# Loading x of tiles 0 and 1 and the first weights through one DMA queue in order of use, with chunks in four parts and seven idle matmuls

## The chip, the cores and the metric

The kernel runs on the 8 cores of one Trainium2 chip; every core has one of the eight sequences of the batch. The time of a run is the device time in microseconds (us) of the slowest core. Executions fall in two states, whatever the kernel: in the slow one the cores of one die, or of both, show a lower granted TensorE clock and the run is some per cent longer, up to 3317 us. Only fast runs are compared.

Each run also lists the span of each core, from its first to its last instruction. I use two figures beside the time: the span of the slowest core, which makes the time, and the mean span of the eight cores, which is less at the mercy of one core.

## The reference

One residual block of a streaming encoder, on x of 8 sequences x 4096 frames x 1024 channels. Only its first part bears on the change:

```python
def reference(x, norm_ffn1, ffn1_w_gate, ffn1_w_up, ffn1_w_down, ...):
    # macaron first half-step FFN
    x = x + 0.5 * swiglu(rmsnorm(x, norm_ffn1[l]), ffn1_w_gate[l], ffn1_w_up[l], ffn1_w_down[l])
    # ... gated attention and gMLP mixers, second half-step FFN ...
    return rmsnorm(x, norm_final)

def swiglu(h, w_gate, w_up, w_down):
    return (jax.nn.silu(h @ w_gate) * (h @ w_up)) @ w_down
```

## The kernel before

A core works on tiles of 512 frames; x of a tile lies in SBUF as 128 partitions x 8 rows x 512 columns of f32 (2.10 MB). A gate-and-up weight chunk ("fsrc") is 128 x 4096, written as bf16 (1.05 MB) into the ring of weight buffers RING. Its eight slices of 512 columns go with the eight rows of x: 32 matmuls for one chunk and one tile. Tiles 0 and 1 start together: chunk 0 for tile 0, chunk 1 for tile 0, then the same two chunks for tile 1.

The weights are issued by GpSimd (the software DMA queue), x by SyncE (a hardware queue). `p.dma` and `p.add` record an operation with what it reads and writes, and a helper derives the semaphore waits from that. So `reads=[("X", 0, 4)]` on a weight load is a pure wait: GpSimd may not issue chunk 1 before row 4 of x of tile 0 has landed.

```python
# pump(): weight chunk k into its ring slot
if k < 2:
    for j in range(4):                       # chunks 0 and 1 in four parts
        part = (slice(None), slice(j * 1024, (j + 1) * 1024))
        p.dma("pool", lambda e, o=dst[part], i_=src[part]: e.dma_start(out=o, in_=i_),
              reads=[("X", 0, 4)] if k else (), writes=res[2 * j:2 * j + 2], sem=f"first{k}{j}")
else:                                        # later chunks in one piece
    p.dma("pool", lambda e, dst=dst, src=src: e.dma_start(out=dst, in_=src),
          reads=[("X", 1, 3)] if k == 2 else (), writes=res, sem=f"slotq{i}")
# ... cut ...
# gu_chunk(), tile 0 with chunk 0
for kc in range(8):
    nraw(t, 0, kc)                           # VectorE: XT = X * gain, f32 to bf16
    for j in range(4):
        mm(j, kc)                            # TensorE
    if kc:
        nsq(t, kc - 1, "dve")                # ScalarE squares, VectorE adds into ACC
nsq(t, 7, "dve")
nstat(RS[t], ("RS", t))                      # TensorE sums ACCR over partitions; ScalarE makes YA
# ... while chunk 1 goes on: scalings and additions for tile 1, one row at a time
nraw(1, 0, d)                                # VectorE
nsq(1, d)                                    # ScalarE squares, GpSimd adds
# ... cut ...
# the start of the program
load_x(0, False)                             # SyncE, eight rows
pump(2)                                      # chunks 0 and 1
load_x(1, False, lambda d: c1[5])            # SyncE waits for the third part of chunk 1
pump()                                       # chunks 2, 3 and 4
```

So the kernel before sets the order x of tile 0 with chunk 0, chunk 1, x of tile 1, chunk 2 by three waits: GpSimd for x of tile 0, SyncE for chunk 1, GpSimd for x of tile 1.

Of the kernel before, what the change touches and what calls it, by code (L numbers as in the profile page):

```python
# [17 lines left out]
T = 512  # L18
NT = S_LEN // T
NGR = 46  # L20
NSEM = 12
EPS = 1e-6
R_MAX = 1e18
BIAS_MAX = 10.0
# [6 lines left out]
def _keep_at():  # L31

    at = {("ffs", 0, f2): int(n < 4) for n, f2 in enumerate(F2J)}
    at |= {("wds", 0, d): 1 for d in range(8)}
    at |= {("wis", g): n for g, n in zip((4, 3, 2, 0, 1), (1, 0, 1, 0, 1))}
    at |= {("mgs", d): n for d, n in enumerate((0, 1, 1, 2, 0, 1, 2, 1))}
    at |= {("wos", 0): 1, ("wos", 1): 2}
    at |= {("ffs", 1, f2): n for f2, n in zip(F2, (1, 2, 0, 2, 1, 2, 1, 0, 2, 1, 2))}
    at |= {("wds", 1, d): n for d, n in enumerate((1, 2, 2, 1, 0, 2, 1, 2))}
    return at  # L40


KEEP_AT = _keep_at()


class _Op:
# [156 lines left out]
def build_nc(n_tiles=NT):  # L203
# [28 lines left out]
    with ExitStack() as st:  # L232
# [5 lines left out]
        def bank(i):  # L238
            return PS[i // 2][:, (i % 2) * 512:(i % 2 + 1) * 512]
# [56 lines left out]
        def run(p, dry):  # L296
# [4 lines left out]
            place = {}  # L301
# [22 lines left out]
            def pump(stop=1 << 30):  # L324
                while nxt[0] < min(stop, len(chunk_order)) and (general[0] or nxt[0] < fast_len[0]):
# [17 lines left out]
                    if chunk not in converted:  # L343
                        u = uses.get(chunk, 0)
                        uses[chunk] = u + 1
                        if k < 2:
                            for j in range(4):
                                part = (slice(None), slice(j * 1024, (j + 1) * 1024))
                                p.dma("pool", lambda e, o=dst[part], i_=src[part]: e.dma_start(out=o, in_=i_),
                                      reads=[("X", 0, 4)] if k else (), writes=res[2 * j:2 * j + 2], sem=f"first{k}{j}")  # L350
                        else:
                            p.dma("pool", lambda e, dst=dst, src=src: e.dma_start(out=dst, in_=src),
                                  reads=[("X", 1, 3)] if k == 2 else (), writes=res, sem=f"slotq{i}")
                        if u >= KEEP_AT[chunk]:
                            converted.add(chunk)
                            pending_wb[k] = (chunk, scr, dst, i)
                    else:
                        p.dma("sp", lambda e, dst=dst, scr=scr: e.dma_start(out=dst, in_=scr),
                              reads=[("SCR", chunk)], writes=res, sem=f"slot{i}")
# [24 lines left out]
                    del live[k]  # L384
                    pump()

            def load_x(t, paced=True, after=None):
                b = t % 3
                step = 4 if paced else 1
                for d in range(0, 8, step):  # L390
                    p.dma("sp", lambda e, d=d: e.dma_start(out=X[b][:, d:d + step, :],
                                                        in_=x_d[:, d:d + step, t * T:(t + 1) * T]),
                          reads=[after(d)] if after else [], writes=[("X", b, i) for i in range(d, d + step)],
                          sem=f"x{b}{d}", paced=paced)

            dn = [0]

# [648 lines left out]
                    pass  # L1046

            p.dma("act", lambda e: e.dma_start(out=G4[:], in_=g4_d), writes=["G4"], sem="c0")
            load_x(0, False)
            if not dry:  # L1050
                pump(2)
                c1 = place[1][1]
                load_x(1, False, lambda d: c1[5])
                pump()
            p.add("dve", lambda e: e.memset(ONESR[:].bitcast(F32), 1.0), writes=["ONESR"])
            p.add("dve", lambda e: e.memset(EPSB[:], EPS), writes=["EPSB"])
            p.add("dve", lambda e: e.memset(NHALF[:], -0.5), writes=["NHALF"])
# [178 lines left out]
```

## Time and profile before

| | before |
|---|---|
| first three timed runs | 2795.04, 2960.86, 3316.71 us (one fast, two slow) |
| fast runs, all later calls (27) | 2787.2 to 2796.3 us, median 2790.8 |
| TensorE busy in the profiled run | 97% of 2786.6 us |
| first real matmul, mean of 8 cores | 9.9 us |
| first statistics matmul (tile 0) | 22.4 us |
| second statistics matmul (tile 1), from which TensorE is full | 46.3 us |

The page counts busy time by engine, divides the span into 40 slices, and follows back the chain that ended last; the prediction shows those lines. The lines of GpSimd (POOL) are its time-ordered view on core 5: start, duration, engine and line, what, how many; in brackets the idle time before and what ended it.

```profile
1.56 2.32 POOL L349 DMA_DIRECT2D RING<-fsrc  x4 [0.87 <-POOLq L204]
16.13 2.21 POOL L349 DMA_DIRECT2D RING<-fsrc  x4 [12.25 <-DMA X<-xT]
29.49 1.58 POOL L352 DMA_DIRECT2D RING<-fsrc  x3 [11.15 <-DMA X<-xT]
31.07 1.29 POOL L477 TENSOR_TENSOR ACC<-ACC,TG 128x512 f32<-128x512 f32 x1
```

Two of the three ordering waits are here (12.25 and 11.15 us for X).

### The profile page before, as it was taken

What the parts mean: (1) busy time and instruction counts of PE and PEld (TensorE: products, weight loads), DVE (VectorE), ACT (ScalarE), POOL (GpSimd) and SP (SyncE); (2) the same over time, 40 slices, a digit from 0 to 9 for tenths busy, and PEclk for the clock granted to TensorE, in tenths of its full rate; (3) what the DMA queues carried; (4) which work ended last, traced back from release to release, by engine and by line L of the source; (5) the groups of instructions that cost most, each with busy time, mean ns of one, the idle gap of its engine ahead of it and who ended that gap; (6) DMA issues with size and microseconds to landing.
All of it is one profiled execution on the core that took longest, in us unless ns stands there. A gap on an engine that the chain in (4) does not pass through costs nothing.

```text
span 2786.6 us, 38337 instructions; the slowest of 8 cores (2777.5 to 2786.6 us)
## 1 busy us (share of the span) xinstructions
PE 2702.4 (97%) x13034; PEld 1209.5 (43%) x13034; DVE 1183.2 (42%) x1940; ACT 910.7 (33%) x1466; POOL 311.5 (11%) x356
## 2 busy tenths in 40 slices
PE   7998999999999999999999999999999999999997
PEld 2443444434444444444444444444444444444343
DVE  5643543435334453344533445424443244455332
ACT  3323432225322353223432244322442225314321
POOL 2001120101111011110011001010011101100111
PEclk9999999999999999999999999999999999999998
DMA  9868989977797556974344634446344453443352
GB/s 190 188 124 178 212 179 178 201 241 149 185 202 222 166 144 175 231 231 148 133 151 144 212 129 136 152 149 210 122 142 150 159 169 130 144 148 123 119 186 79
DMA packets 87124, 461.91 MB, mean 166 GB/s; under 512 B 9224, under 2 KB 9224, under 8 KB 55056
## 3 DMA queue, kind: packets, MB, share of 16 engines
q1 hardware_dynamic: 70656, 365.68, 38.6%
q0 software_dynamic: 16128, 93.69, 21.1%
q8 instruction: 112, 1.84, 0.3%
q14 instruction: 84, 0.69, 0.1%
q10 hardware_dynamic: 144, 0.02, 0.0%
HBM read 488.03 MB, written 65.01 MB: 198 GB/s over the span
## 4 chain that ended last, share of the span: by engine, by line
PE 88%; DMA 5%; DVE 3%; ACT 2%; issue 2%; DVEq 0%; SPq 0%; POOL 0%; ACTq 0%; POOLq 0%
PE ps L547 40%; PE ps L618 19%; PE ps L930 8%; PE ps L671 6%; PE ps L684 4%; PE ps L940 4%; PE ps L959 4%; PE ps L835 2%; DMA ffs<-RING 2%; PE ps L812 1%; ACT E L818 1%; DMA RING<-fsrc 1%; DMA RING<-wd 1%; DMA RING<-ffs 1%; DMA X<-xT 1%
## 5 line engine op out<-in xcount | busy, mean ns | idle before, releaser
L547 PE MATMUL ps<-XT,RING 128*128 128x512 bf16 x5632 | 1232.5, 380 | 25.4 <-DMA RING<-fsrc 10.6
L547 PEld LDWEIGHTS ps<-XT,RING 128*128 128x128 bf16 x5632 | 547.6, 98 | 691.8 <-issue 41.3
L618 PE MATMUL ps<-HT,RING 128*128 128x512 bf16 x2656 | 607.6, 380 | 9.2 <-DVE HT L571 7.1
L477 POOL TENSOR_TENSOR ACC<-ACC,TG 128x512 f32<-128x512 f32 x174 | 224.2, 1289 | 1710.0 <-ACT TG L474 1709.6
L571 DVE TENSOR_TENSOR HT<-ps,TG 128x512 bf16<-128x512 f32 x332 | 229.2, 690 | 386.6 <-PE ps L547 338.9
L618 PEld LDWEIGHTS ps<-HT,RING 128*128 128x128 bf16 x2656 | 252.9, 98 | 317.4 <-issue 36.3
L474 ACT ACTIVATE TG<-X 128x512 f32<-128x512 f32 x224 | 140.1, 627 | 404.0 <-DVE X L624 329.5
L930 PE MATMUL ps<-XT,RING 128*128 128x512 bf16 x1024 | 241.9, 379 | 2.8 <-ACT TG L935 1.6
L554 ACT ACTIVATE TG<-ps 128x512 f32<-128x512 f32 x154 | 91.9, 597 | 402.0 <-PE ps L547 372.6
L560 ACT ACTIVATE TG<-ps 128x512 f32<-128x512 f32 x154 | 91.9, 597 | 372.6 <-PE ps L547 366.3
L556 DVE SCALAR_TENSOR_TENSOR TG<-TG,ps 128x512 f32<-128x512 f32 x154 | 105.8, 687 | 246.7 <-ACT TG L554 201.2
L823 DVE TENSOR_TENSOR E<-E,EB 128x1024 bf16<-128x1024 bf16 (+1 forms) x240 | 120.1, 504 | 168.3 <-ACT E L818 157.7
L624 DVE SCALAR_TENSOR_TENSOR X<-ps,X 128x512 f32<-128x512 f32 x128 | 88.3, 690 | 239.2 <-PE ps L618 238.0
L818 ACT ACTIVATE E<-ps 128x1024 bf16<-128x1024 f32 (+3 forms) x156 | 152.5, 983 | 67.2 <-PE ps L812 62.8
L671 PE MATMUL ps<-XT,RING 128*128 128x512 bf16 x768 | 168.4, 379 | 0.0
L944 DVE SCALAR_TENSOR_TENSOR TG<-TG,ps 128x512 f32<-128x512 f32 x128 | 87.2, 686 | 159.4 <-PE ps L940 122.9
L930 PEld LDWEIGHTS ps<-XT,RING 128*128 128x128 bf16 x1024 | 98.5, 98 | 127.1 <-issue 12.9
L935 ACT ACTIVATE TG<-ps,BG 128x512 f32<-128x512 f32 x128 | 87.2, 687 | 194.9 <-PE ps L930 182.8
L499 DVE SCALAR_TENSOR_TENSOR XT<-X,G,RSTD 128x512 bf16<-128x512 f32 x176 | 124.6, 745 | 36.3 <-ACT RSTD L492 36.3
L671 PEld LDWEIGHTS ps<-XT,RING 128*128 128x128 bf16 x768 | 75.2, 98 | 90.6
L684 PE MATMUL ps<-RING,XT 128*128 128x512 bf16 x512 | 114.3, 379 | 0.0
L959 PE MATMUL ps<-HT,RING 128*128 128x512 bf16 x448 | 99.0, 379 | 2.1 <-DVE HT L949 2.1
(101 smaller groups left out, 1524.4 us busy)
## 6 DMA issues: line engine op xcount, KB each, us to landing
RING<-ffs SPq DMA_DIRECT2D x126, 1024.0 KB, 4.9
RING<-wds SPq DMA_DIRECT2D x93, 704.0 KB, 4.8
RING<-fsrc POOLq DMA_DIRECT2D x38, 1024.0 KB, 14.7
RING<-mgs SPq DMA_DIRECT2D x48, 768.0 KB, 4.2
RING<-wis SPq DMA_DIRECT2D x32, 1024.0 KB, 4.8
RING<-wd POOLq DMA_DIRECT2D x35, 704.0 KB, 13.8
ffs<-RING SPq DMA_DIRECT2D x22, 1024.0 KB, 12.9
out<-X SPq DMA_DIRECT2D x32, 512.0 KB, 5.5
```

The lines of the kernel that those rows point to most:

```text
L474: p.add("act", lambda e: e.activation(out=buf[:], in_=src, func=AF.Square, scale=1.0 / 32.0), reads=[xres], writes=[bres])
L477: p.add(eng, lambda e: e.tensor_tensor(out=ACC[:], in0=ACC[:], in1=buf[:], op=ALU.add), reads=["ACC", bres], writes=["ACC"])
L499: p.add("dve", lambda e: e.scalar_tensor_tensor(out=dst, in0=src, scalar=G4[:, which * 8 + d:which * 8 + d + 1], in1=RSTD[:], op0=ALU.mult ...
L547: p.add("pe", lambda e: e.matmul(bank(b), lhsT=Wc[:, kc * 512 + j * 128:kc * 512 + (j + 1) * 128], rhs=xt[:, kc, :], start=(kc == 0), stop ...
L571: p.add("dve", lambda e: e.tensor_tensor(out=dst, in0=bank(bu), in1=buf[:], op=ALU.mult), reads=[rb(bu), bres], writes=[dres])
L618: p.add("pe", lambda e, fc=fc, W=W, by=by, hap=hap: e.matmul(bank(by), lhsT=W[:, fc * 128:(fc + 1) * 128], rhs=hap, start=(fc == 0), stop= ...
L671: p.add("pe", lambda e, kc=kc, W=W, b=b, cc=cc: e.matmul(bank(b), lhsT=W[:, kc * 512 + cc * 128:kc * 512 + (cc + 1) * 128], rhs=XT[t % 2][ ...
L684: p.add("pe", lambda e, kc=kc, W=W, b=b, s=s: e.matmul(bank(b), lhsT=XT[t % 2][:, kc, s * 128:(s + 1) * 128], rhs=W[:, kc * 512:(kc + 1) * ...
L818: p.add("act", lambda e, j=j, sl=sl, qa=qa, col=ok_col(): e.activation(out=E[:, sl, :, qa:T], in_=PS[1 + j][:].rearrange("p (h c) -> p h c ...
L823: p.add("dve", lambda e, sl=sl, q0=q0, q1=q1, u0=u0: e.tensor_tensor(out=E[:, sl, :, q0:q1], in0=E[:, sl, :, q0:q1], in1=EB[:, 2 * hp:2 * ...
L930: p.add("pe", lambda e, kc=kc, W=W, bgt=bgt, j=j: e.matmul(bank(bgt), lhsT=W[:, j * 1024 + kc * 128:j * 1024 + (kc + 1) * 128], rhs=XT[t % ...
L959: p.add("pe", lambda e, dc=dc, W=W, by=by, d4=d4: e.matmul(bank(by), lhsT=W[:, (d4 * 8 + dc) * 128:(d4 * 8 + dc + 1) * 128], rhs=m[:, dc, ...
```

## The change

The intent is to put everything that the start needs into one queue in the order in which it is used, so that the queue's order takes the place of the waits, with smaller pieces that can be used sooner; and to wake TensorE's clock with seven matmuls on zeros while there is nothing to do.

```diff
+X_FIRST = {(0, 0): [(0, 0, 1)], (0, 1): [(0, 1, 2), (0, 2, 4)], (0, 2): [(0, 4, 6)], (0, 3): [(0, 6, 8)],
+           (2, 0): [(1, d, d + 2) for d in range(0, 8, 2)]}
...
-                        if k < 2:
+                        if k < len(F2J):
                             for j in range(4):
+                                for x in X_FIRST.get((k, j), ()):
+                                    load_x_part(*x)
                                 part = (slice(None), slice(j * 1024, (j + 1) * 1024))
                                 p.dma("pool", lambda e, o=dst[part], i_=src[part]: e.dma_start(out=o, in_=i_),
-                                      reads=[("X", 0, 4)] if k else (), writes=res[2 * j:2 * j + 2], sem=f"first{k}{j}")
+                                      writes=res[2 * j:2 * j + 2], sem=f"first{k % 6}{j}")
                         else:
                             p.dma("pool", lambda e, dst=dst, src=src: e.dma_start(out=dst, in_=src),
-                                  reads=[("X", 1, 3)] if k == 2 else (), writes=res, sem=f"slotq{i}")
+                                  writes=res, sem=f"slotq{i}")
...
+            def load_x_part(t, d0, d1):
+                p.dma("pool", lambda e: e.dma_start(out=X[t][:, d0:d1, :], in_=x_d[:, d0:d1, t * T:(t + 1) * T]),
+                      writes=[("X", t, d) for d in range(d0, d1)], sem=f"xf{t}{d0}")
...
-            load_x(0, False)
             if not dry:
-                pump(2)
-                c1 = place[1][1]
-                load_x(1, False, lambda d: c1[5])
                 pump()
+            p.add("dve", lambda e: e.memset(HT[:, 0, :], 0.0), writes=[("HT", 0)])
+            for _ in range(N_WARM):
+                p.add("pe", lambda e: e.matmul(bank(7), lhsT=HT[:, 0, 0:128], rhs=HT[:, 0, :], start=True, stop=True),
+                      reads=[("HT", 0)], writes=[rb(7)])
```

`len(F2J)` is 11, so all of the first eleven chunks now go in four parts.

## The prediction

> **What bounds the kernel now.** I read the list of cores first, because two of the three timed runs before were slow. In the profiled run all eight cores lie between 2777.5 and 2786.6 us with granted clocks of 0.993 to 0.996, so this trace is of the fast state. Then I read the head of the page.
>
> ```profile
> span 2786.6 us, 38337 instructions; the slowest of 8 cores (2777.5 to 2786.6 us)
> PE 2702.4 (97%) x13034; PEld 1209.5 (43%) x13034; DVE 1183.2 (42%) x1940; ACT 910.7 (33%) x1466; POOL 311.5 (11%) x356
> PE   7998999999999999999999999999999999999997
> ```
>
> TensorE is the bound: 97% busy, and only the first of the forty slices (0 to 70 us) stands at 7, apart from a dip in the fourth and the tail. The change touches that first slice and nothing else, so the next view is the chain that ended last, its pieces in order of time.
>
> ```profile
> 3.42 14.21 DMA X<-xT
> ...
> 45.72 117.44 PE ps L547 x544
> 177.35 27.14 PE ps L618 x125
> ```
>
> Up to 17.6 us the path is the load of x. From 45.7 us on it is plain matmul work for 117 us. Between lies the start-up, which the time-ordered view of TensorE shows (start, duration, what; in brackets the idle time before it and what ended it).
>
> ```profile
> 10.58 6.77 PE L547 MATMUL ps<-XT,RING 128*128 128x512 bf16 x20 [10.58 <-DMA RING<-fsrc]
> 18.36 3.02 PE L547 MATMUL ps<-XT,RING 128*128 128x512 bf16 x12 [1.01 <-DVE XT L504]
> 21.82 0.47 PE L488 MATMUL ps<-ACCR,ONESR 128*128 128x512 f32 x1 [0.44 <-DVE ACCR L480]
> 22.14 0.60 PE L547 MATMUL ps<-XT,RING 128*128 128x512 bf16 x2
> 23.22 6.63 PE L547 MATMUL ps<-XT,RING 128*128 128x512 bf16 x30 [0.48 <-ACT YA L490]
> 32.81 3.27 PE L547 MATMUL ps<-XT,RING 128*128 128x512 bf16 x8 [2.95 <-DVE XT L504]
> ...
> 43.60 1.89 PE L547 MATMUL ps<-XT,RING 128*128 128x512 bf16 x8 [2.04 <-DVE XT L504]
> ```
>
> TensorE first has work at 10.58 us, when the first weights land; tile 0's statistics (L488) run at 21.82; tile 1's first chunk trickles between 32.8 and 45.5, each step waiting for VectorE (XT, L504). The busy times up to 45.56 add to about 27.1 us, so 18.5 us are idle. **That is the most that any start-up change can return: 18.5 / 2786.6 = 0.66%**, plus some 3.5 us of half-speed matmuls (about 17 of them at 0.43 us where others take 0.216).
>
> Why tile 1 trickles is in VectorE's own time-ordered view:
>
> ```profile
> 23.90 0.69 DVE L563 TENSOR_TENSOR TG<-ps,YA 128x512 f32<-128x512 f32 x1 [2.23 <-ACT YA L492]
> 30.40 0.69 DVE L571 TENSOR_TENSOR HT<-ps,TG 128x512 bf16<-128x512 f32 x1
> 31.01 2.05 DVE L504 TENSOR_SCALAR XT<-X,G 128x512 bf16<-128x512 f32 x2
> 35.09 2.97 DVE L504 TENSOR_SCALAR XT<-X,G 128x512 bf16<-128x512 f32 x2
> ```
>
> From 23.90 us, where YA (the root-mean-square factor of tile 0) is ready, VectorE and ScalarE pass the results of chunk 0 and 1 back and forth, and tile 1's scalings sit in that program order. No bracket of this stretch names x: in the list of waits VectorE's six waits for x add to 12.2 us, and all lie before 18 us (2.94, 0.26, 5.24, 1.71, 1.05, 0.95). So **x of tile 1 is already in time; the chain from YA to full flow, 23.9 to 45.6 us, is not a DMA chain**.
>
> **What the Trainium skill says.** "DMA: Bandwidth & Descriptors", section "Queues, rings and completion order": every DMA engine takes turns between the queues that have work, packet by packet. The trace agrees: from 6 to 10 us the hardware queue moved 0.36 MB of x and the software queue 0.33 MB of weights. The same page, "Issuing engines are not separate DMA queues": all issuers share the same 16 engines, so one queue instead of two buys order, not bandwidth. "TensorE: Matmul & The Clock Gate", "Part 1: The HAM clock gate", has the array at half clock until it has been busy for about 3.4 us; here the first ten matmuls came 0.43 us apart, until 15 us. "SBUF — State Buffer", "SBUF: two separate sides": VectorE and GpSimd can lock each other out of a shared port. The trace fits: a scaling takes 0.48 us alone, and two took 2.97 us where GpSimd additions of 1.26 us ran beside them.
>
> **The change part by part.** The order listing of the two programs shows that the work is unchanged but for 7 matmuls, one memset and more, smaller DMA issues. GpSimd now issues 29 DMAs before its first addition (x of tile 0 in five, x of tile 1 in four, chunks 0 to 4 in four parts each), where it issued 11 in three groups with waits for x.
>
> 1. *Issue cost.* One GpSimd issue took 0.55 us (2.32 us for four). 29 x 0.55 = 16 us, from 1.6 to 17.6 us. GpSimd's first addition is at 31.07 us before, so this is hidden if nothing blocks. For chunks 5 to 10 it is 4 x 0.55 instead of 0.53 us each, beside TensorE-bound work: nothing.
>
> 2. *First chunk.* Rates in the stretch table: x alone 357 GB/s (26 to 30 us), weight parts alone 201 GB/s written (20 to 23 us). x of tile 0 is 2.10 MB, 5.9 us; chunk 0 is 1.05 MB written, 5.2 us; sum 11.1 us. Mixed on two queues they took about 14.5 us (2.7 to 17.2). In one ordered queue I take 11.1 us at best and 15 us if the mixing loss stays; the start is near 3.0 us, the last x pair lies 1.3 us before the end and is seen about 1 us after it has moved: 13.8 to 17.3 us, against 17.7 before. First matmul: x row (0.7 us) and one part (1.3 us) after 3.0 us plus completion, so 6 to 7 us instead of 10.6. From the last x to L488 took 4.1 us (17.7 to 21.8; square, add, add). So L488 moves from 21.8 to between 18 and 21.4; central 19, a gain of nearly 3 us.
>
> 3. *Second chunk and tile 1.* Their DMAs now follow without the gaps (engines 0.68 busy at 16 to 18 and 22 to 24 us). Chunk 1 lands near 20 to 23 us; its 32 matmuls (7 us) then end by 26 to 28 instead of 29.85 and are not asked for by VectorE until about 30. x of tile 1 lands at 26 to 29, needed from 28 on. Both are off the path, without much to spare.
>
> 4. *Seven idle matmuls.* 7 x 0.43 = 3.0 us, from about 1.5 to 4.5 us, before any data. They may bring the clock up for chunk 0, but chunk 0 is paced by arrivals (a part and an x pair, 2.8 us, for eight matmuls that take 1.7 us warm and 3.4 us cold). In the old run the cold matmuls had been caught up before the last x. Worth 0 to 1 us.
>
> 5. *Rest.* The YA-to-full-flow chain of 21.7 us (23.9 to 45.6) keeps its instructions and length. Later waits are released by TensorE's own progress and shift along. Sum: about **3 us earlier**, a profiled span near 2783.5 us. The two fast runs on hand are 2789.63 and 2795.04 us, mean 2792; minus 3 is **2789 us**.
>
> **The rivals.** (a) *The order works better than I think*, and tile 1 also flows: the chain after YA shortens as well, and 6 to 12 us come back, 2780 us. For it: 18.5 us are idle. Against: VectorE's brackets name ScalarE and GpSimd there, and not one DMA. (b) *The deep software queue blocks GpSimd.* With 29 DMAs ahead, GpSimd might have to wait for space and come late to its additions for tile 1, and VectorE's L480 and TensorE's second L488 behind them: 5 to 15 us lost, 2797 to 2807 us. Before, GpSimd never had more than about four issues of this kind waiting at once in the start, so the profile does not exclude it; 15%. (c) *No gain*: x through the software queue is slower than its 357 GB/s, or the parts arrive no sooner, and chunk 0 ends at 18 us as before: 2792 us. The low 158 GB/s at 4 to 10 us, which two queues alone may not explain, speaks for this; 25%. (d) *Given back later*: one 6.2 us wait for weights near 590 us, where the DMA engines are full; but the transfers in front of it are released by TensorE, so it moves with it.
>
> **Range and chances.** Among fast runs I expect 2775 to 2803 us: fast executions of the same kernel differ by 5 us, and the rivals reach 2780 and 2807. The measured median can fall in the slow state, which two of three timed runs before did (2960.86 and 3316.71), whatever the change does; so the range on record goes up to that slow median: **2772 to 2965 us**. The predicted time itself is for a fast run. Since even all idle start-up time is 0.66%, a change of over 2% between fast runs is all but excluded: faster 0.02, same 0.96, slower 0.02.
>
> **What would show each step right or wrong.** Step 2: in the time-ordered view TensorE's first real matmul at 6 to 7 us and the first statistics matmul at 18 to 21.4 us. Step 3: no wait for x or weights between the two statistics matmuls. Step 1: 29 GpSimd issues done by about 18 us, and the first GpSimd addition not later than 31 us. Step 5: from YA to full flow again 21 to 22 us, then a path with the same pieces, each about 3 us earlier. It is wrong if full flow begins before 38 us or after 46 us, or if a new wait stands after it.

## The result and the profile after

| runs right after the prediction | before | after |
|---|---|---|
| all timed runs, median | 2879.49 us (4; two slow) | 2791.77 us (4; all fast) |
| fast runs | 2795.04, 2798.13 | 2788.84, 2791.03, 2792.51, 2793.79 |
| ratio after / before | | 0.9982, 95% interval 0.9958 to 1.0006: same |

A ratio here is the mean time of one kernel's fast runs over that of the other's of the same rounds, so it is not quite the ratio of the medians in the table. In all later calls together, 8 fast runs of the kernel after have a median of 2789.7 us (2786.3 to 2793.9), and 27 of the kernel before 2790.8 us. I counted a fast run here only where no core's mean granted clock was under 0.988; that leaves out two runs of before, 2817 and 2824 us, that passed as fast with one die at 0.98. The mean slowest span is 2788.3 us after and 2787.9 us before, the mean of all cores 2783.8 us in both. **So the work on the cores takes as long as before.** The 1.1 us between the medians is less than the remainder outside the spans changed: time minus slowest span is 2.9 to 3.4 us in every run of before and 1.5 to 1.8 us in every run of after.

The page of the profiled run after, head lines; this is core 0, the slowest:

```profile
span 2787.3 us, 38178 instructions; the slowest of 8 cores (2781.2 to 2787.3 us)
PE 2690.8 (97%) x12782; PEld 1210.4 (43%) x13041; DVE 1183.5 (42%) x1941; ACT 910.7 (33%) x1466; POOL 331.7 (12%) x392
PE   7998999999999999999999999999999999999997
```

The first slice still stands at 7. The first long piece of the chain that ended last was `X<-xT` from 3.42 to 17.63 us in before. It is now:

```profile
6.69 15.31 DMA RING<-fsrc
```

**The start is still a DMA chain, but its last link is weights instead of x, and it ends at 22.00 us instead of 17.63.** TensorE in order of time shows the same (core 0):

```profile
1.88 3.02 PE L1064 MATMUL ps<-HT 128*128 128x512 bf16 x7 [1.88 <-DVE NHALF L1068]
8.46 1.87 PE L558 MATMUL ps<-XT,RING 128*128 128x512 bf16 x4 [3.57 <-DMA RING<-fsrc]
...
19.21 1.89 PE L558 MATMUL ps<-XT,RING 128*128 128x512 bf16 x8 [1.36 <-DMA RING<-fsrc]
22.25 1.89 PE L558 MATMUL ps<-XT,RING 128*128 128x512 bf16 x8 [1.15 <-DMA RING<-fsrc]
23.78 0.58 PE L499 MATMUL ps<-ACCR,ONESR 128*128 128x512 f32 x1
...
34.75 3.01 PE L558 MATMUL ps<-XT,RING 128*128 128x512 bf16 x8 [2.82 <-DVE XT L515]
38.67 5.33 PE L558 MATMUL ps<-XT,RING 128*128 128x512 bf16 x16 [0.91 <-DVE XT L515]
45.54 1.89 PE L558 MATMUL ps<-XT,RING 128*128 128x512 bf16 x7 [1.54 <-DVE XT L515]
47.19 0.47 PE L499 MATMUL ps<-ACCR,ONESR 128*128 128x512 f32 x1
```

The idle matmuls run from 1.88 us, the first real one at 8.46, and the last eight of chunk 0 wait for weights until 22.25. Only then the statistics matmul, which stands behind them in program order, can run. From there to full flow (the second statistics, after which TensorE has work without a gap) TensorE waits for no DMA on this core; the brackets name VectorE, as before.

Why was nothing gained although the order is now the right one? The table by stretches has the answer. Its columns are the stretch, its length, busy us of PE, PEld, DVE, ACT and POOL with counts, the granted clock, the busy share of the 16 DMA engines, and what they moved. Before (core 5):

```profile
0.00:4.00 4.00, 0.00 (x0) 0.00 (x0) 0.18 (x3) 0.00 (x0) 2.51 (x8) 1.00 0.36 119
4.00:10.00 6.00, 0.00 (x0) 0.00 (x0) 0.97 (x2) 2.43 (x3) 0.00 (x0) 1.00 1.01 158
10.00:16.00 6.00, 5.42 (x15) 2.00 (x16) 2.48 (x5) 1.58 (x3) 0.00 (x0) 1.00 1.05 235
16.00:20.00 4.00, 2.99 (x14) 0.96 (x12) 3.05 (x7) 2.09 (x4) 2.21 (x4) 1.00 0.88 184
```

After (core 0):

```profile
0.00:4.00 4.00, 2.12 (x6) 0.76 (x7) 0.64 (x4) 0.00 (x0) 2.60 (x8) 1.00 0.14 26
4.00:10.00 6.00, 2.43 (x7) 0.56 (x5) 0.48 (x1) 1.91 (x2) 6.00 (x11) 0.84 1.01 195
10.00:16.00 6.00, 3.91 (x10) 1.07 (x10) 3.14 (x7) 2.36 (x5) 6.00 (x11) 0.50 1.04 220
16.00:20.00 4.00, 2.64 (x9) 0.80 (x8) 1.52 (x3) 0.57 (x2) 2.70 (x6) 0.71 1.03 175
```

In both, the DMA engines are full from 4 us on. The old order left almost no gap to win (0.88 from 16 to 20 us); what the new one wins there it loses in the first 4 us, where it moves 26 GB/s instead of 119. Summed over the four rows, before moved 3.57 MB by 20 us (119 x 4 + 158 x 6 + 235 x 6 + 184 x 4, in kB), after 3.29 MB. These are two different cores; in the mean of all eight, from the packet records, it is 3.34 MB before (0.37 of it in the first 4 us) and 3.37 MB after (0.12). The clock column is to be read with care: it shows 1.00 where the trace has no clock record yet. On core 5 of before the first record begins at 15.1 us, and until then matmuls came 0.43 us apart, where later ones come 0.21 us apart.

The trace also records each DMA packet with its size and the time its engine took. Means over the 8 cores, packets that start before 21 us:

```
                              bytes    ns each    one load: packets x ns / 16 engines
before  weights (software q)  2048     242        512 x 242 / 16 = 7.7 us   (chunk 0)
before  x       (hardware q)  2048     108       1024 x 108 / 16 = 6.9 us   (x of tile 0)
after   weights (one queue)   2048     247        512 x 247 / 16 = 7.9 us
after   x       (one queue)   4096     226        512 x 226 / 16 = 7.2 us
```

Chunk 0 and x of tile 0 need 14.6 us of all 16 engines before and 15.1 us after. Counted from some 4 us that ends at 19 us in either order. These packet times are no fixed prices: in before, weight packets that started from 4 to 6 us took 368 ns each, those from 12 to 14 us 193 ns. The sum says how long the loads held the engines in this stretch, and that the two orders hold them alike. **An order cannot shorten the sum of what has to arrive before the first statistics.**

The landing records (each transfer's 16 engines report one by one) agree. Mean of 8 cores, in us, median engine / last engine:

```
                        before           after
first x (row 0)          4.0 /  4.5       5.6 /  6.4
last x of tile 0        17.4 / 19.3      17.3 / 19.3
last part of chunk 0    15.8 / 17.8      19.3 / 20.7
last part of chunk 1    25.9 / 26.6      26.1 / 27.8
last x of tile 1        34.0 / 34.9      32.5 / 35.6
```

The last x comes at the same time to 0.1 us, the last weights of chunk 0 2.9 us later. For tile 1 the median engine is 1.5 us sooner, but the last engine, which the kernel waits for, is 0.7 us later. In the one queue that is not emptied between the stages the engines have run apart: 3.1 us between median and last, against 0.9 us before.

### The profile page after: what moved, and what is told of

Same layout as the page of the kernel before. It is cut to its first block, busy times and chain, and to the rows that moved or that the text cites. A ratio compares the mean times of both kernels' runs of the same rounds, so it can differ in the third digit from the quotient of the medians.

```text
span 2787.3 us, 38178 instructions; the slowest of 8 cores (2781.2 to 2787.3 us)
## 1 busy us (share of the span) xinstructions
PE 2690.8 (97%) x12782; PEld 1210.4 (43%) x13041; DVE 1183.5 (42%) x1941; ACT 910.7 (33%) x1466; POOL 331.7 (12%) x392
## 4 chain that ended last, share of the span: by engine, by line
PE 86%; DMA 4%; DVE 3%; ACT 3%; issue 3%; POOL 0%; DVEq 0%; ACTq 0%; SPq 0%; POOLq 0%
PE ps L558 40%; PE ps L629 18%; PE ps L941 8%; PE ps L682 5%; PE ps L695 4%; PE ps L951 4%; PE ps L970 4%; PE ps L846 2%; DMA ffs<-RING 1%; DMA RING<-fsrc 1%; PE ps L823 1%; ACT E L829 1%; DMA RING<-wd 1%; DVE X L635 1%; DVE E L834 1%
## 5 line engine op out<-in xcount | busy, mean ns | idle before, releaser
L558 PEld LDWEIGHTS ps<-XT,RING 128*128 128x128 bf16 x5632 | 547.6, 98 | 686.2 <-issue 34.9
L629 PE MATMUL ps<-HT,RING 128*128 128x512 bf16 x2589 | 600.8, 380 | 15.2 <-DVE HT L582 8.4
L488 POOL TENSOR_TENSOR ACC<-ACC,TG 128x512 f32<-128x512 f32 x174 | 223.9, 1287 | 1719.5 <-ACT TG L485 1719.0
L970 PE MATMUL ps<-HT,RING 128*128 128x512 bf16 x440 | 98.5, 379 | 2.5 <-DVE HT L960 2.1
```

What stands on the lines that cost most here:

```text
L488: p.add(eng, lambda e: e.tensor_tensor(out=ACC[:], in0=ACC[:], in1=buf[:], op=ALU.add), reads=["ACC", bres], writes=["ACC"])
L558: p.add("pe", lambda e: e.matmul(bank(b), lhsT=Wc[:, kc * 512 + j * 128:kc * 512 + (j + 1) * 128], rhs=xt[:, kc, :], start=(kc == 0), stop ...
L629: p.add("pe", lambda e, fc=fc, W=W, by=by, hap=hap: e.matmul(bank(by), lhsT=W[:, fc * 128:(fc + 1) * 128], rhs=hap, start=(fc == 0), stop= ...
L970: p.add("pe", lambda e, dc=dc, W=W, by=by, d4=d4: e.matmul(bank(by), lhsT=W[:, (d4 * 8 + dc) * 128:(d4 * 8 + dc + 1) * 128], rhs=m[:, dc, ...
```

## The experiments

Fifteen runs were made, in four groups on one chip each. In the table, times are fast runs with no core's clock under 0.988; a single run is not a measurement of one per mille. The last four columns are from the profiled run: first real matmul, first and second statistics matmul, and the difference, each a mean over the 8 cores; where the profiled run fell in the slow state (no_warm, x_old_way) over the four cores of the undisturbed die.

| kernel | fast runs | median us | slowest span, mean | first matmul | stat. 1 | stat. 2 | difference |
|---|---|---|---|---|---|---|---|
| before | 27 | 2790.8 | 2787.9 | 9.9 | 22.4 | 46.3 | 23.9 |
| after | 8 | 2789.7 | 2788.3 | 9.1 | 22.7 | 45.8 | 23.1 |
| after_again | (in after) | | | 8.7 | 21.9 | 45.0 | 23.1 |
| after_five | (in after) | | | 8.6 | 22.5 | 45.6 | 23.1 |
| no_warm | 2 | 2792.0 | 2790.4 | 8.4 | 23.6 | 46.9 | 23.3 |
| warm_only | 1 | 2791.1 | 2788.2 | 9.8 | 22.6 | 47.0 | 24.4 |
| x_old_way | 5 | 2791.8 | 2791.6 | 10.1 | 22.6 | 51.0 | 28.4 |
| resync | 1 | 2800.1 | 2798.3 | 8.5 | 22.2 | 57.9 | 35.7 |
| x0_sp | 1 | 2790.6 | 2789.1 | 9.9 | 27.6 | 50.9 | 23.4 |
| x_first | 5 | 2788.7 | 2787.3 | 15.2 | 22.4 | 45.8 | 23.4 |
| half_w0 | 1 | 2790.3 | 2788.8 | 8.5 | 22.7 | 45.7 | 23.0 |
| dve_adds | 4 | 2785.9 | 2785.2 | 8.8 | 22.3 | 45.2 | 23.0 |
| whole_chunks, whole_again, whole_five | 10 | 2785.1 | 2784.6 | 8.7 | 22.0 | 45.0 | 23.0 |
| chunk2_free | 3 | 2805.1 | 2801.8 | 9.7 | 22.6 | 62.4 | 39.8 |
| before_sems | 1 | 2791.2 | 2788.1 | 10.4 | 22.4 | 47.2 | 24.8 |

My theory after the result was this: the start is bound by engine time of the DMAs, so an order in one queue does what the old waits did, no more; the chain between the two statistics is one of VectorE, ScalarE and GpSimd, about 23 us long whenever GpSimd is free in time. The rival: the order does help, and something else in the change (the many issues, the quarters, the idle matmuls) takes the gain back.

### The change again, and each part alone

**after_again** is the kernel after, unchanged, with five rounds.

> The changed kernel once more, unaltered, for a closer ratio of the times. My theory after the first trace: the shared queue does not bring x of tile 0 or the first weights sooner (mean over the cores of the last x of tile 0: 19.3 us in both kernels), so the statistics of tile 0 come no earlier (22.7 against 22.4 us, mean of eight cores) and only some cores gain, because x of tile 1 is no longer late there (second statistics at 45.8 us mean, 47.2 latest, against 46.3 and 48.3). That is worth 0.5 to 1 us, ratio 0.9996 to 0.9998. Rival: the change is worth the 5 us (0.9982) that the first fast runs showed; then the ratio stays at 0.998 and its interval excludes 1.

The ratio was 0.9979 (0.9911 to 1.0046), too wide to tell theory from rival. It counts the 2824 us run of before as fast; without that run the means are 2790.6 and 2791.7 us, a ratio of 0.9996, as the theory said. The 5 us, with two fast runs of before, did not come again.

**no_warm** and **warm_only** take the idle matmuls out of the change, and put them alone into the kernel before.

```diff
# no_warm, against after
-N_WARM = 7
+N_WARM = 0
# warm_only, against before
+            p.add("dve", lambda e: e.memset(HT[:, 0, :], 0.0), writes=[("HT", 0)])
+            for _ in range(7):
+                p.add("pe", lambda e: e.matmul(bank(7), lhsT=HT[:, 0, 0:128], rhs=HT[:, 0, :], start=True, stop=True), ...)
```

> Takes away only the seven idle matmuls. My theory: they are worth nothing, because on the profiled core the granted clock still stood at one half from 8 to 18 us and the chunk is paced by arrivals; the statistics of tile 0 stay at 22.4 to 23 us (mean) and the ratio to before stays within 0.0005 of that of the changed kernel. Rival: they shorten the start, then the first statistics move to 23.5 us or later and the ratio rises by 0.0005 or more.

> The kernel before plus only the memset and the seven idle matmuls. Expected: first and second statistics as before (22.4 and 46.3 us in the mean, to 1 us). It also asks what else differs: in all runs of the kernel before the measured time is 3.0 to 3.2 us longer than the slowest core's span, in all runs of the changed one and its variants 1.5 to 1.8 us. If the idle matmuls caused that, it is 1.5 here; if it goes with the quarter chunks and their number of semaphores (87 in this kernel as before, 98 and more in the others), it stays at 3.

no_warm: ratio 0.9982 (0.9896 to 1.0068); without the 2824 us run of before 1.0001, from two fast runs. Its profiled run fell in the slow state; on the undisturbed die the first statistics came at 23.6 us and the second at 46.9, 1 us later than in the profiled runs of the change, whose cores differ among themselves by more than that. By the numbers this is on the side of the rival (23.5 us or later, 0.0005 more), but four cores and two runs do not settle it. warm_only had its second statistics at 47.0 us, no sooner than before. So alone the matmuls gained nothing, and within the change something like 1 us is possible and not shown. On core 0 they end at 4.90 us, TensorE then idles 3.57 us, and in the rows of after above the granted clock is 0.84 from 4 to 10 us and 0.50 from 10 to 16. The clock records of the eight cores say why so little came of it: on four of them (0, 1, 2, 7) the clock rose, at 4.6 to 5.6 us, and was back at one half 3.4 us later, at 8.0 to 9.0 us, just as the first real matmuls began (8.3 to 9.2 us); on the other four the first record is at 12.8 us or later, after the first eight real matmuls at 0.43 us each.

**x_old_way** keeps the quarters of all eleven chunks and the idle matmuls, but loads x on SyncE with the old waits.

```diff
# against after
-                                for x in X_FIRST.get((k, j), ()):
-                                    load_x_part(*x)
+                                      reads=([("X", 0, 4)] if k == 1 else [("X", 1, 3)] if k == 2 else ()),
+            load_x(0, False)
+                pump(2)
+                c1 = place[1][1]
+                load_x(1, False, lambda d: c1[5])
```

> Undoes one part: x of tiles 0 and 1 on the SP queue with the waits of before; the quarter chunks and the seven idle matmuls stay. If the queue order is what the change lives from, first real matmul goes back from 9.1 to about 9.9 us, the second statistics from 45.8 to about 46.3 us in the mean with 48 on the latest cores, and the ratio to before is 1.000. If the quarter chunks or the idle matmuls are what helps, the ratio stays below 0.999 like that of the changed kernel.

On the undisturbed die the second statistics came at 51.0 us, 5 us later than before. GpSimd on core 5, which is of that die, shows why:

```profile
32.41 6.76 POOL L354 DMA_DIRECT2D RING<-fsrc  x12 [12.88 <-DMA X<-xT]
38.88 1.59 POOL L487 TENSOR_TENSOR ACC<-ACC,TG 128x512 f32<-128x512 f32 x1
```

Twelve quarter issues take 6.76 us where three whole ones took 1.58, and the first addition for tile 1 begins at 38.88 instead of 31.07 us. In the kernel after the same twelve issues are over by 18.7 us, 14 us before the first addition. **So quarters do cost GpSimd, and what makes them harmless is that no wait for x stands before them.** The ratio was 0.9986 (0.9937 to 1.0034; without the 2824 us run of before 1.0005), while the mean of all cores' spans rose by about 4 us (2787.9 against 2783.8).

### One queue, but emptied between the stages

**resync** is the change with three waits of GpSimd added: chunk 1 waits for the end of chunk 0, x of tile 1 for the end of chunk 1, chunk 2 for x of tile 1.

```diff
# against after
+                                sync = {(1, 0): [res_of[0][6]], (2, 0): [("X", 1, 7)]}.get((k, j), [])
-                                      writes=...
+                                      reads=sync, writes=...
# load_x_part
+                      reads=[res_of[1][6]] if (t, d0) == (1, 0) else [],
```

> The changed kernel with three waits in GpSimd's issue order: the first part of chunk 1 waits until the last part of chunk 0 has landed, x of tile 1 until the last part of chunk 1 has, chunk 2 until the last x of tile 1 has. My theory of the long tails: with a queue that never runs dry the sixteen engines drift apart (last minus median landing grows from 0.8 us to 3.1 us at the last x of tile 1 and 3.8 us at chunk 4, against 0.9 and 1.0 us before, where waits stopped the queue). With the waits the tail falls to 1 us for chunk 1, x of tile 1 and after, at the price of about 1.5 to 2 us of empty queue at each wait. Rival: the tail comes from the small parts or from the software queue itself; then it stays at 2 us and more behind the waits.

It separates two things. The tails shrank: from median to last engine 0.7 us for x of tile 1 (39.5 / 40.2) against 3.1 us in the change. So emptying the queue between the stages takes the tail away. That a full queue by itself makes it is not shown: from 45 to 64 us twelve quarters ran in this kernel through a queue that was not emptied, and their tails stayed at 0.8 to 1.2 us. And the gaps, with the issues behind them, cost more than the tail: x of tile 1 was there only at 40.2 us, and GpSimd's additions began at 48.26 us (core 0) behind twelve issues. The second statistics matmul was 12 us late and the run 2800.1 us.

### Which of the loads goes first

**x0_sp** puts x of tile 0 back on SyncE and leaves the rest of the deep queue without waits.

```diff
# against after
-X_FIRST = {(0, 0): [(0, 0, 1)], (0, 1): [(0, 1, 2), (0, 2, 4)], (0, 2): [(0, 4, 6)], (0, 3): [(0, 6, 8)],
-           (2, 0): [(1, d, d + 2) for d in range(0, 8, 2)]}
+X_FIRST = {(2, 0): [(1, d, d + 2) for d in range(0, 8, 2)]}
+            load_x(0, False)
```

> The changed kernel with x of tile 0 alone back on the SP queue; weights and x of tile 1 stay in one queue on GpSimd. If the shared queue orders the first transfers usefully, the last x of tile 0 comes later than its 18.8 to 19.4 us (mean) and the first matmul later than 8.7 to 9.1 us. If one queue only trades a later start of its first bytes (x row 0 at 5.6 to 6.3 us against 4.5 us on SP) for the order, the last x stays within 0.7 us of 19 us and the first matmul comes about 0.8 us later, with no effect on the second statistics (45 to 46 us).

The last x of tile 0 landed at 25.4 us (last engine) instead of 19.3, and both statistics moved by 5 us, with the same 23.4 us between them. So order is worth something: without either the waits or the shared queue it is lost.

**x_first** loads x of tile 0 alone, before any weights, and has the statistics before the last matmuls of chunk 0.

```diff
# against after
+                                      reads=[("X", 0, 3)] if k + j == 0 else [],     # chunk 0 waits for x
+            load_x(0, False)                                                          # on SyncE
# gu_chunk: all scalings and squares of tile 0 first; then the matmuls,
+                        if first == 0 and t == 0 and kc == 5:
+                            nstat(RS[t], ("RS", t))
```

> Built from the changed kernel: x of tile 0 alone first on the SP queue (chunk 0 waits until its fourth row has landed), and the statistics matmul of tile 0 moved ahead of chunk 0's last eight matmuls. My theory: what sets the start of full flow is the time of YA plus a chain of 23 us that no load touches, so YA must come sooner, and in the changed kernel it comes only when x and chunk 0 have both landed. Expected: last x of tile 0 near 11 us instead of 19, first statistics at 18 to 20 us instead of 22, second statistics near 43 us (mean of the cores) instead of 45 to 46, time of fast runs 2 to 3 us below the changed kernel's (ratio to before 0.9985 to 0.9995). Rival: the bytes bound everything, then chunk 0 lands so much later that chunk 1 and x of tile 1 hold up the chain and the second statistics stay at 45 us or later.

x of tile 0 was there at 11.9 us instead of 19.3, and chunk 0 at 20.7, exactly as in the change. The second statistics came at 45.8 us, ratio 0.9998 (0.9984 to 1.0013): the rival held. This is the clearest test of the sum: x comes 7 us sooner and nothing is gained, because the weights come later in its place. Their end is not all of it, though. The first part of chunk 0 landed at 14.9 us instead of 8.9, and on six of the eight cores TensorE then ran the 24 matmuls that stand before the statistics without a wait, in 6.5 to 7.6 us, up to half of them at 0.43 us; there the limit was the first weights and TensorE's own time.

**half_w0** loads only half of chunk 0, and uses that half twice (the result is wrong; relative error 0.059).

```diff
# against after
+                                if k == 0 and j > 1:
+                                    continue
+                    wk = kc % 4 if k == 0 else kc
```

> A wrong result on purpose: the changed kernel without the second half of chunk 0 (1.05 MB less to read; its first half is used twice). My theory: the start is bound by the bytes that must land, whatever the order, so with 0.52 MB less ahead of it the last x of tile 0 lands 1.5 to 2 us sooner (near 17 us, mean of cores), chunk 1 about 3.5 us sooner, the first statistics come at 20 to 20.5 us and the second, 23 us later, at 43 to 43.5 us instead of 45 to 46. Rival: the 23 us are bound by chunk 1 or x of tile 1, then the second statistics move by the whole 3.5 us to 42 us; or GpSimd or VectorE bound the whole start, then they stay at 45 us.

The median engine had the last x 2.0 us sooner (15.3 instead of 17.3) and x of tile 1 4.0 us sooner (28.5 instead of 32.5), so bytes do count. But the last engine was hardly sooner (19.2 and 34.3 us against 19.3 and 35.6). On five cores the second statistics came at 43.2 to 44.4 us, on cores 1, 2 and 6 at 47.3 to 50.0. The gain is there in the median engine and is lost to the slowest ones: at the last x of tile 1 two of the sixteen reports came 10 to 12 us after the median on cores 1 and 2, and one 9.5 us after it on core 6. One run, 2790.3 us.

### The waits that the change replaced

**chunk2_free** is the kernel before with one thing gone: GpSimd's wait for x of tile 1 ahead of chunk 2. I suspected that this wait cost the kernel before its small lag (46.3 against 45.0 to 45.8 us).

```diff
# against before
-                                  reads=[("X", 1, 3)] if k == 2 else (), writes=res, sem=f"slotq{i}")
+                                  writes=res, sem=f"slotq{i}")
```

> The kernel before without GpSimd's wait for x of tile 1 ahead of chunk 2, nothing else changed. Theory (the small gain of the change comes from GpSimd being free for its additions): GpSimd has issued chunks 2 to 4 by about 26 us, the cores on which the two statistics matmuls lay 25 to 26 us apart fall to 23 us, mean of the second one 0.5 to 1.2 us sooner than before's 46.3 us. Rival: chunk 2 now shares the engines with x of tile 1, which lands 2 us or more later than 34.0 us, and the second statistics matmul is as late as before or later.

The rival was right, and by far: the second statistics came at 62.4 us, 16 us later, and the kernel became slower, ratio 1.0044 (1.0024 to 1.0065), 2805.1 us. VectorE on core 2 is now waiting for x of tile 1 in the stretch where it did not before:

```profile
41.38 0.49 DVE L504 TENSOR_SCALAR XT<-X,G 128x512 bf16<-128x512 f32 x1 [9.10 <-DMA X<-xT]
47.33 0.49 DVE L504 TENSOR_SCALAR XT<-X,G 128x512 bf16<-128x512 f32 x1 [5.46 <-DMA X<-xT]
...
52.09 0.49 DVE L504 TENSOR_SCALAR XT<-X,G 128x512 bf16<-128x512 f32 x1 [2.16 <-DMA X<-xT]
```

The last x of tile 1 landed at 54.6 us instead of 34.9. The packet records from 30 to 45 us, mean of 8 cores, say how two queues share an engine: 275 packets of the weights' queue (8192 bytes, 757 ns each) beside 264 of x's (2048 bytes, 125 ns). One packet against one packet, so four times the bytes and six times the engine time for the weights. That is what the Trainium skill states in "DMA: Bandwidth & Descriptors", "Queues, rings and completion order", and the lesson is its consequence: **between these two queues the one with the larger packets won, and a wait, or one common queue, kept the urgent small rows ahead.**

This also settles what the old waits were: not idle time to be saved, but the order itself. The one queue of the change keeps that order, and gets the same time for it.

### Is GpSimd the limit between the two statistics?

**dve_adds** gives the additions of tile 1 to VectorE, on top of whole_chunks below.

```diff
# against whole_chunks
-                                nsq(1, d)
+                                nsq(1, d, "dve")
```

> The same with tile 1's six additions of squares on VectorE instead of GpSimd. My theory of the 23 us from first to second statistics, the same in every variant whose GpSimd is free: VectorE's eight scalings of tile 1 took 1.5 + 3.0 + 1.3 + 1.9 = 7.7 us beside GpSimd's additions where 0.48 us each would be 3.9; on VectorE the additions cost 6 x 0.69 = 4.1 us, part of it in the gaps in which VectorE waits for ScalarE. Expected: 20 to 22 us instead of 23.0, second statistics near 43 us, 1 to 3 us gained in the span. Rival: VectorE is full there, the additions cost what the lock cost, and it stays at 23 us or grows.

Ratio 0.9976 (0.993 to 1.0022); the difference between the statistics stayed at 22.95 us. Taking GpSimd out of the chain does not shorten it. That does not clear GpSimd: one cost went and another came, as the rival said. A pair of tile 1's scalings, 2.97 us in the prediction's lines beside GpSimd's additions, has here (core 0) become two of this kind:

```profile
35.17 0.48 DVE L517 TENSOR_SCALAR XT<-X,G 128x512 bf16<-128x512 f32 x1
```

In the mean of the cores the eight scalings took 3.8 us together instead of 7.7 in whole_chunks, and the six additions, now VectorE's, took that time back: VectorE was busy for 15.2 us between the two statistics, 15.5 in whole_chunks.

### The quarters of the later chunks

**whole_chunks** is the change with chunks 2 to 10 in one piece, as before. **whole_again** is the same with five rounds, and **whole_five** and **after_five** put it and the change side by side on the same chip.

```diff
# against after
-                        if k < len(F2J):
+                        if k < 2:
                         ...
                         else:
+                            for x in X_FIRST.get((k, 0), ()):
+                                load_x_part(*x)
```

> The changed kernel with only chunks 0 and 1 in four parts, the others whole. Theory: the quarter chunks are no help by themselves (with the old order they held GpSimd for 6.8 us ahead of its additions and full flow began at 51 us); in the queue of the changed kernel they are issued long before and cost nothing, so here the second statistics stay at 45 to 46 us. Rival: quarters bring chunk 2 in sooner and help; then a wait for chunk 2 appears after the second statistics. Measured time minus slowest span: tells whether 91 semaphores give 1.5 or 3 us.

> The one-queue kernel with chunks 2 to 10 whole again, timed closely, since its single run was the fastest yet (2784.5 us, mean of the cores 2781.2). If that was more than luck: fast runs 4 to 6 us below those of before, mean of the cores 2781 to 2782 against 2783.4 to 2784.2. If the quarters are neutral, as its second statistics suggest (44.8 us against 45.0 and 45.8 of the changed kernel), the spans come back to 2783 us and only the 1.5 us outside the span remain.

> The changed kernel once more, on the same chip and beside the same runs of the kernel before as the two kernels that follow. If the small gain of the whole chunks is real, the fast runs here lie at 2789 to 2793 us, mean of the cores' spans 2784 to 2786 us. Time minus the slowest span 1.5 to 1.8 us.

> One queue, chunks 2 to 10 whole. Theory: the quarters of chunks 2 to 10 cost 2 to 5 us somewhere after 46 us, so the fast runs here lie at 2784 to 2788 us and the mean of the cores' spans at 2781 to 2783 us, 2 us or more under the changed kernel beside it. Rival: the earlier gap was chance between calls; then both kernels agree within 1.5 us. First statistics matmul at 21.5 to 22.5 us, second at 44.5 to 45.5 us in the mean of the cores for both.

whole_chunks ran at 2784.5 us. whole_again had a ratio of 0.9996 (0.9946 to 1.0045), blurred by one run of 2809.3 us, and one of before of 2817.2, that count as fast with a die at clock 0.98; its other four were 2784.1, 2785.0, 2785.3 and 2790.6 us, and without the two runs the ratio is 0.9982. whole_five was at 0.9983 (0.9968 to 0.9998) of before, beside after_five at 0.9990 (0.9973 to 1.0007): 2785.0 to 2789.4 us (5 fast) against 2786.3 to 2790.5 us (4 fast). **So one queue with whole later chunks is 0.17% under before**, and about 1.5 us of these 4.7 us is the remainder outside the spans. Against the change its fast runs overlap (means 2786.4 and 2789.0 us), so that it beats the change is likely and not shown.

Why it would be sooner than the change is only partly clear. Their second statistics lie 0.5 us apart. The mean of the cores' spans in the last call differs by 0.8 us (2783.2 and 2782.4), where the theory had asked for 2 us or more, but the mean slowest span by 2.6 us (2787.4 and 2784.8). In the profiled run of after_five the slowest core stands alone:

```profile
core 2: 2788.4 us, clock 0.993
core 3: 2782.2 us, clock 0.994
```

and its TensorE shows a late start:

```profile
24.20 3.57 PE L558 MATMUL ps<-XT,RING 128*128 128x512 bf16 x8 [2.92 <-DMA RING<-fsrc]
27.21 0.99 PE L499 MATMUL ps<-ACCR,ONESR 128*128 128x512 f32 x1
...
50.75 0.47 PE L499 MATMUL ps<-ACCR,ONESR 128*128 128x512 f32 x1
```

Of the 16 reports of the last part of chunk 0 on this core, fourteen had come by 20.3 us and two came at 23.9 and 24.0. Two late DMA engines on one core made the time of the whole chip. On the other seven cores the second statistics matmul lies at 44.0 to 45.5 us. whole_five had its worst core at 47.3 us, so such stragglers happen there too; that whole chunks make them rarer is not shown.

**before_sems** asked whether the 1.5 us outside the spans come from the number of semaphores: before, with more of them (110 in all).

```diff
-NSEM = 12
+NSEM = 20
```

> The kernel before with nothing changed but the number of semaphores that its slots rotate through (110 in the program instead of 87). If the 1.5 us by which measured time and slowest span lie closer together in the changed kernel come with the count of semaphores, the difference here is 1.5 us instead of 3.0; if they come with something else in the change, it stays at 3.0. Start-up and span as before.

The remainder stayed at 3.1 us. warm_only (2.9) and chunk2_free (3.0 to 3.1) keep it too; every kernel that has either the quarters of the later chunks or x on GpSimd has 1.5 to 1.8. What makes it is open.

## Why the prediction was right or wrong

**The frame was right.** TensorE is the bound, the start is all that the change touches, 0.66% is the ceiling, and "same" held: 0.9982.

**Step 1 (issue cost) was right.** The 29 issues ended at 18.7 us on core 0 (predicted 17.6 to 18), the first addition came at 33.1 us behind 14.4 us of idle time. Rival (b), a blocked GpSimd, did not happen.

**Step 2 (first chunk) is the step that failed.** "First matmul ... 6 to 7 us" was 8.6 to 9.1 us in the means of three runs; "L488 moves from 21.8 to between 18 and 21.4" was 21.9 to 22.7 us against 22.4 before. One ordered queue that follows the use was there; the sum was mis-sized, and the wait that ends last was another. I had chunk 0 complete 11.1 us after 3.0 us, at 14.1 us at best (18 us if the mixing loss stayed); it was complete at 20.7 us. The 6.6 us between split by the landing records of after like this:

- The first row of x was predicted at 3.0 + 5.9 / 8 = 3.7 us and landed at 5.6 us on the median engine: 1.8 us.
- The other seven rows of x took 5.7 us, predicted 5.9 x 7 / 8 = 5.2 us: 0.5 us.
- The four parts of chunk 0 took 2.3, 1.9, 1.8 and 2.0 us, together 8.0 us, predicted 5.2 us: 2.8 us. The rate of 201 GB/s that I took was that of core 5 alone from 20 to 23 us; over the eight cores of the same trace it was 71 to 209 GB/s there, 138 in the mean. A weight packet of 2048 bytes cost 247 ns of its engine here.
- The last engine came 1.4 us after the median one, which I had not counted.

The terms add to 6.5 us. Two readings led there. I took the 14.5 us of the mixed queues against the 11.1 us of the sum for a loss that one queue could win back (and in step 3 the share of 0.68 in a 2 us stretch for a gap), where the engines were at 0.93 over the whole of 4 to 20 us in the mean of the cores before (1.01 after). And I followed only the last x to the statistics, although the last part of chunk 0 now stands behind it in the same queue and its eight matmuls stand before the statistics matmul: the wait for x had become a wait for weights. I also read core 5 alone. The last scaling that waited for x began there at 17.7 us; the mean of eight cores was 18.2. And "x of tile 1 is already in time" holds there, while on cores 1, 4 and 6 of the same trace ScalarE waited 0.6 to 1.8 us for it.

**Step 3 (second chunk and tile 1) was right in its consequence and wrong in its times.** On core 0 the only wait for a DMA between the two statistics is one of 0.18 us of ScalarE; on cores 2, 5 and 7 TensorE waited 0.6 to 1.3 us for chunk 1, and the stretch was no longer for it (23.0 to 23.1 us). But chunk 1 landed at 27.8 us, not 20 to 23, and x of tile 1 at 35.6 us, not 26 to 29.

**Step 4 (idle matmuls, 0 to 1 us) agrees with what was measured**: alone they gained nothing, and without them the start of the change was about 1 us later, which is within the spread of its cores. The Trainium skill, "TensorE: Matmul & The Clock Gate", "Part 1: The HAM clock gate", asks for about 3.4 us of work; these took 3.0 us on core 0, and an idle stretch of 3.6 us followed. The clock rose on four cores of eight, and fell again as the first real matmuls began.

**Step 5 (the rest) was right in the chain and wrong in the shift.** From YA to full flow it is 21.5 us on core 0 (25.98 to 47.50), predicted 21.7. But with step 2 gone there was no 3 us to carry on: full flow began at 47.50 us there, later than the 46 us that the prediction had named as its sign of being wrong (45.8 us in the mean of the cores), and the slowest span stayed at 2788 us. The 2789 us is close to the measured 2789.7 by luck: it was 3 us less than a mean of two runs, and what came was no gain on the cores and 1.5 us less outside the spans, which the prediction did not have.

**The rivals.** (c), no gain because the parts arrive no sooner, is what happened, and I had given it 25%, though chunk 0 came not at 18 us as before but at 20.7; my reason for it, the low 158 GB/s with two queues mixed, was half of the cause. That rate is low because weight packets are slow (242 ns), and they are as slow in one queue (247 ns). (a) did not come. (d) was not needed: what later stretches did to a shift can be seen in chunk2_free, where 16 us at the start became 14 us at the end, so nothing downstream hides or returns much.

The small gain that is left, 0.5 to 1.3 us in the second statistics, goes with the shorter stretch between them: 23.1 us in all three runs of the change, 23.9 before, where three cores had 25.0 to 26.2. On one of these, core 1, the trace of before shows GpSimd's part in it: its wait for x and three issues end at 37.5 us, its six additions then follow each other without a pause, and VectorE waits for them twice, 1.28 and 1.35 us; the second wait stands just before the second statistics.

```profile
46.81 0.69 DVE L480 TENSOR_TENSOR ACCR<-ACC,TG 128x512 fp32r<-128x512 f32 x1 [1.35 <-POOL ACC L477]
```

On cores 4 and 6 no such wait stands; there ScalarE waited for x of tile 1 itself (0.57 and 1.48 us; 1.80 in sum on core 1). So late x and a late GpSimd are both in it, and their shares stay open: the run meant to separate them, chunk2_free, lost the order as well.

## What to carry to other kernels

Before an order of loads is improved, add up the engine time of everything that must land before the first dependent step (packets x time of one packet / 16, the time taken from the same stretch and from all cores); if that sum fills the stretch, another order of the same loads has little to win. A wait that looks like idle time may be what keeps a small urgent load ahead of a large one in another queue, so it can be dropped only where a common queue takes over its work. And on eight cores look at the last engine on the worst core, since that is what the time is made of.

## What the Trainium skill lacked or had wrong

- "DMA: Bandwidth & Descriptors" has nothing on how far the 16 engines of one queue can run apart when the queue is not emptied between stages: 3.1 us between the median and the last engine for x of tile 1 in the change, 0.7 us where the queue was emptied between stages (resync). Its section "Latency and other measured facts" says that DMA engines 7 and 15 are usually slower; on core 2 of after_five two of sixteen came 3.6 us after the rest, which would fit, but the records here do not name the engine.
- The same page gives the turns packet by packet, which chunk2_free confirms (275 packets against 264), but not the consequence for the bytes: whole chunks of 8192-byte packets took four times the bytes of x's 2048-byte rows, and x of tile 1 landed 20 us later.
- No page that I read prices a packet of a weight load that changes f32 to bf16: 2048 bytes written took 242 to 247 ns of an engine, 108 ns for 2048 bytes of plain x.
- No page that I read explains the remainder between the slowest span and the time, 2.9 to 3.4 us for some kernels here and 1.5 to 1.8 us for others.
